# Weight sums of a Winograd-form squared-ReLU layer: sign changes, and two of four sums made by accumulating DMA transfers

## The chip, the cores and the metric

The kernel runs on one core of a Trainium2 chip. The core has a matrix engine (TensorE, "PE" in the profile, with its weight loads as "PEld"), a vector engine (VectorE, "DVE"), an activation engine (ScalarE, "ACT"), a general engine (GpSimd, "POOL") and a synchronisation engine (SyncE, "SP") that here issues nearly all DMA transfers. The metric is device time in microseconds (us) of one execution.

## The reference

A trunk of two residual layers on 512 tokens of width 1024, all in float32. Layer 0 mixes tokens with chunked band attention, layer 1 with a gated linear recurrence. Behind each mixer stands a dense squared-ReLU layer, which is what the change is about:

```python
def sq_relu_mlp(h, w1, w2):
    z = jax.nn.relu(jnp.einsum('bsd,df->bsf', h, w1))
    return jnp.einsum('bsf,fd->bsd', z * z, w2)

def reference(x, norm_mix, norm_mlp, ...):
    h = x
    for layer in range(DEPTH):
        hn = rmsnorm(h, norm_mix[layer])
        ...
        h = h + mix
        h = h + sq_relu_mlp(rmsnorm(h, norm_mlp[layer]), mlp_w1[layer], mlp_w2[layer])
    return rmsnorm(h, norm_final)
```

The hidden width is 4096, so `w1` is 1024 x 4096 and `w2` is 4096 x 1024.

## The kernel before

**Precision.** A float32 product is made of three matmuls of a reduced format (float32r): each operand is rounded to a high part, and what is left over is its low part. So every unit of weights, 128 partitions by 1024 elements (512 KB), is loaded by a transfer of SP, rounded by ScalarE (line 141, tile `wh`), and its low part is formed by VectorE (line 144, tile `wl`). A function `fetch` does this for the next unit of a written-out list, `plan`. `want` hands units to TensorE in that order, and fetches until five units (four outside these layers, three in a last round) are ready beyond those it hands out.

**The squared-ReLU layer.** The second product is done in four rounds `p`. A round takes 1024 rows of `w2` and all its 1024 columns, as four blocks of 512 x 512: "11" and "12" are the left and right columns of the first 512 rows, "21" and "22" those of the second. The activations of the round form four blocks too: two halves of the tokens (256 each) by two halves of the rows. With four blocks a side the round uses Winograd's form of Strassen's product: seven block products in place of eight, paid for with sums of blocks. On the activations' side these are `s1` to `s4` (lines 686 and 730 to 733). On the weights' side they are

- t1 = 12 - 11, written over block 12,
- t2 = 22 - t1, written over block 22 after block 22 itself has been used,
- t3 = t2 - 11, written over block 11,
- t4 = 21 - t2, written over block 21.

Each is made by VectorE in two halves (128 x 1024 elements each) at line 139, in `fetch`, right before the rounding cast of that half. The blocks are loaded by SP at line 129, eight transfers of 512 KB a round, when `fetch` comes to the unit "11". Each of the four blocks has one buffer (tags `b11`, `b21`, `b12`, `b22`), so a load waits until the round before has done with it. The buffers of "12" and "22" first hold the residual, turned, at the start of a layer (`turn`, line 636: 32 small transfers), and only then the first round's blocks.

**The order of the work.** In a round TensorE computes the second half of the first product's columns (`up`, j = 4 to 7), then the seven products: "11", "21" (with the activations' "12"), t1, "22", t2, t3, t4. Between the last four it computes the first half of the next round's columns (`ahead`), except in the last round. The activations come out of PSUM through a ReLU and a square on ScalarE (lines 655 and 656), and each block or sum of them is split into high and low part (`split`, lines 679 and 680). Products are read back from PSUM by VectorE (`read`, line 643) as d = acc x r + d, where r is the per-token factor of the norm, `rq`. The engines each run their own queue in order. What stands in what order in a queue is decided when the program is built, by a planner that goes by its own costs, and the order of the source breaks ties. GpSimd has no work in these layers.

Of the kernel before, what the change touches and what calls it, by code (L numbers as in the profile page):

```python
# [10 lines left out]
F32 = mybir.dt.float32  # L11
F32R = mybir.dt.float32r
AF = mybir.ActivationFunctionType
ALU = mybir.AluOpType

P = 128
# [5 lines left out]
U = 256  # L22
# [13 lines left out]
def f(ap):  # L36
    return ap.bitcast(F32)
# [3 lines left out]
def trunk(ctx: ExitStack, tc: tile.TileContext, xT, cols, gfin, win, wqkv, wo, rwin, rga, rgx, rwo, w1, w2, out):  # L41
    nc = tc.nc
    V, S, G, PE = nc.vector, nc.scalar, nc.gpsimd, nc.tensor

    per = ctx.enter_context(tc.tile_pool(name="per", bufs=1))
# [6 lines left out]
    def mmp(name):  # L52
        return ps.tile([P, T], F32, name=name, tag="mm")
# [20 lines left out]
    spare = per.tile([P, 1], F32, name="spare")  # L74
    rt = per.tile([P, 4], F32, name="rt")
    rq = per.tile([P, 4], F32, name="rq")
    fs = per.tile([P, 8], F32, name="fs")
    sp4 = per.tile([P, KT], F32, name="sp4")
    sp8 = per.tile([P, KT], F32, name="sp8")
# [19 lines left out]
    raws, start_ = {}, []  # L99

    def fetch():
        i = state["next"]
        state["next"] += 1
        kind, nk, srcs = plan[i]
        pool = wsp
        if state["more"] is not None and i < state["end"]:
            pool = state["more"] if state["units"] % 7 >= 5 else wsp
            state["units"] += 1
        H = pool.tile([P, 1024], F32R, name=f"wh{i}", tag="wh")
        L = pool.tile([P, 1024], F32R, name=f"wl{i}", tag="wl")  # L110
        n = 1024
        if kind == "plain":
            n = nk * sum(src.shape[1] for src in srcs)
            raw = wraw.tile([P, 1024], F32, name=f"wr{i}", tag="wr")
            rv = raw[:, :n].rearrange("p (k c) -> p k c", k=nk)
            c0 = 0
            for n_, src in enumerate(srcs):
                w = src.shape[1]
                queue = nc.scalar if i == 0 and n_ else nc.sync
                queue.dma_start(rv[:, :, c0 : c0 + w], src.rearrange("(k p) c -> p k c", p=P))  # L120
                c0 += w
        else:
            half, nk = nk, 2
            if kind == "11" and half == 0:
                for name, src in zip(("11", "21", "12", "22"), srcs):
                    both = state["raw"].tile([P, 2, 1024], F32, name=f"b{name}_{i}", tag=f"b{name}")
                    for h in range(2):
                        raws[name, h] = both[:, h]
                        nc.sync.dma_start(
                            raws[name, h].rearrange("p (k c) -> p k c", k=2),  # L130
                            src[h * U : (h + 1) * U].rearrange("(k p) c -> p k c", p=P),
                        )

            at_, x, y = {
                "t1": ("12", "12", "11"), "t2": ("22", "22", "12"), "t3": ("11", "22", "11"), "t4": ("21", "21", "22"),
            }.get(kind, (kind, None, None))
            raw = raws[at_, half]
            if x:
                V.tensor_sub(raw, raws[x, half], raws[y, half])  # L139
        if i:  # L140
            S.copy(H[:, :n], raw[:, :n])  # L141
        else:
            start_.append(V.tensor_copy(H[:, :n], raw[:, :n]))
        low = V.tensor_sub(L[:, :n], raw[:, :n], f(H[:, :n]))  # L144
        if not i:
            start_.append(low)
        state["ready"].append((nk, H[:, :n].rearrange("p (k c) -> p k c", k=nk), L[:, :n].rearrange("p (k c) -> p k c", k=nk)))

    def prefetch(n):
        while len(state["ready"]) < n and state["next"] < len(plan) and state["next"] != state["stop"]:  # L150
            fetch()

    def want(n):
        prefetch(n + state["ahead"])
        got = [state["ready"].pop(0) for _ in range(n)]
        nk = got[0][0]
        return (lambda k, c: got[k // nk][1][:, k % nk, c]), (lambda k, c: got[k // nk][2][:, k % nk, c])
# [64 lines left out]
    def project(accs, cols_, WH, WL, xs, first=True, last=True):  # L222

        for k, (XH, XL) in enumerate(xs):
            for acc, c in zip(accs, cols_):
                mm3(acc, WH(k, c), WL(k, c), XH, XL, first and k == 0, last and k == len(xs) - 1)
# [383 lines left out]
    def mlp(ly, norm):  # L610
        with ExitStack() as mctx:
# [6 lines left out]
            dt = {(t, c): res[:, t, c] for t in range(4) for c in range(2)}  # L618
# [6 lines left out]
            def turn():  # L625
                blocks = [sr.tile([P, 2, 4, KT, 32], F32, name=f"turned{ly}{h}", tag=f"b{n}2") for h, n in enumerate((1, 2))]
                for k in range(KT):
                    for h in range(2):
                        V.transpose(
                            blocks[h].rearrange("p t j k a -> p (t j) k a")[:, :, k],  # L630
                            hT[k][:, h * U : (h + 1) * U].rearrange("p (n b) -> p n b", b=32),
                        )
                for h in range(2):
                    for i in range(4):
                        for j in range(4):
                            nc.sync.dma_start(
                                res[32 * j : 32 * j + 32, 2 * h : 2 * h + 2, i // 2, (i % 2) * U : (i % 2 + 1) * U],
                                blocks[h][32 * i : 32 * i + 32, :, j].rearrange("p t k a -> p t (k a)"),
                            )

            def read(acc, t, c):
                d, r = dt[t, c], rq[:, t : t + 1]
                V.scalar_tensor_tensor(d, acc, r, d, ALU.mult, ALU.add)  # L643


# [2 lines left out]
            def up(p, j):  # L648
                if j % 4 == 0:
                    a[p, j // 4] = zp.tile([P, 2, 4, U], F32, name=f"a{ly}{p}{j}", tag=f"a{j // 4}")  # L650
                WH, WL = want(1)
                acc = mmp(f"u{ly}{p}{j}")
                project([acc], [slice(0, P)], WH, WL, xs)
                c = a[p, j // 4][:, :, j % 4, :]
                S.activation(c, acc.rearrange("p (h c) -> p h c", h=2), AF.Relu)  # L655
                S.activation(c, c, AF.Square)  # L656
                if (p, j) == (0, 0):
                    turn()
                if (p, j) == (0, 5):
                    for t in range(4):  # L660
                        for c in range(2):
                            squares(t, c)
                if (p, j) == (0, 6):
                    V.tensor_add(rq, fs[:, 0:8:2], fs[:, 1:8:2])
                    V.tensor_scalar(rq, rq, 1.0 / D, EPS, ALU.mult, ALU.add)
                    V.reciprocal(rq, rq)

            def round_(p):
                A, low, raw = {}, {}, {}
# [7 lines left out]
                def split(n, ks=slice(0, 4)):  # L677
                    H, L = low[n]
                    S.copy(H[:, ks], raw[n][:, ks])  # L679
                    V.tensor_sub(L[:, ks], raw[n][:, ks], f(H[:, ks]))  # L680
# [33 lines left out]
                def step(name, bank, fresh, t0, c):  # L714
                    apart = p == 3 and name != "12"
                    if not apart:
                        product(name, bank, fresh)
                    for t in range(2):
                        if apart:
                            product(name, bank, fresh, ts=(t,))  # L720
                        read(bank[t], t0 + t, c)

                chunks = {5: slice(0, 2), 7: slice(2, 4)} if p < 3 else {5: slice(0, 2), 6: slice(2, 3), 7: slice(3, 4)}
                for j in range(4, 8):
                    up(p, j)
                    raw["12"], raw["22"] = a[p, 1][:, 0], a[p, 1][:, 1]
                    if j in chunks:
                        ks = chunks[j]
                        r = {n: raw[n][:, ks] for n in raw}
                        V.tensor_sub(r["s2"], r["22"], r["s3"])  # L730
                        V.tensor_sub(r["s4"], r["12"], r["s2"])
                        split("12", ks)
                        V.tensor_add(r["s1"], r["s1"], r["22"])

                    if j == (5 if p == 3 else 7):
                        step("11", X, True, 0, 0)
# [33 lines left out]
            def squares(t, c):  # L770
                sq = wk.tile([P, T], F32, name=f"dsq{ly}{t}{c}", tag="nsq", bufs=2)
                S.activation(sq, dt[t, c], AF.Square, accum_out=part(t, c))
# [93 lines left out]
            for j in range(4):  # L866
                up(0, j)
# [11 lines left out]
    def open_x(u):  # L879
        WH, WL = want(1)  # L880
        for i in range(2):
            xbs.append(mmp(f"xb{2 * u + i}"))
            project(xbs[-1:], PAIR[i : i + 1], WH, WL, [(hnH[k], hnL[k]) for k in range(4, KT)], last=False)
            yield

    mlp(0, nm1)


    nm2 = Norm("nm2", C_MLP1, late=True)
    with ExitStack() as rctx:  # L890
# [83 lines left out]
        for u in range(4):  # L974
            WH, WL = want(2 if u > 1 else 1)
            for i in range(2):
                c = 2 * u + i
# [19 lines left out]
        for u in range(4):  # L997
            WH, WL = want(2)
            for i in range(2):
                c = 2 * u + i  # L1000
# [32 lines left out]
        for u in range(2, 4):  # L1033
            WH, WL = want(2)
            for i in range(2):
                m = 2 * u + i
                project([accs[m]], PAIR[i : i + 1], WH, WL, [gd[k] for k in range(KT)])
                ro_out(m)

    mlp(1, nm2)  # L1040


# [39 lines left out]
```

## Time and profile before

| | us |
|---|---|
| runs shown: median (lowest to highest) | 1053.89 (1053.03 to 1054.12) |
| the profiled execution's span, first to last instruction | 1052.7 |
| TensorE busy in it | 1042.4 |
| VectorE busy | 809.2 |
| ScalarE busy | 583.4 |
| GpSimd busy | 9.4 |
| line 139, the weight sums: 64 instructions on VectorE | 76.4 |
| weight blocks of `w2`: 64 transfers of 512 KB, median to landing | 5.6 |

The profiled execution's own time is given by its span alone. The median of the runs is 1.2 us above it. Layer 0's squared-ReLU layer takes the span from about 230 to 570 us, layer 1's from about 715 to the end. A round lasts about 82 us. In the timeline's rows the columns are the start in us, the duration in us, the engine, the line, the operation, the tile written and those read, shapes, and in brackets the engine's idle time just before with what ended it. In rows of groups the numbers behind the bar are busy time in us and the mean of one in ns, then the idle time before them.

### The profile page before, as it was taken

The page shows a single profiled execution, that of the slowest core. Times are in us where ns is not written, and L with a number is a line of the kernel's source. Part 1 is how long each engine was busy: PE and PEld are TensorE (multiplying, and loading weights), DVE is VectorE, ACT ScalarE, POOL GpSimd, SP SyncE. Part 2 cuts the span into 40 slices and gives each one's busy share as a digit, 9 for nine tenths or more (in the row PEclk, how much of TensorE's full clock was granted, in tenths as well). Part 3 has the DMA queues.
Part 4 walks back from the last instruction along what each step waited for, and adds up shares of the span by engine and source line. Part 5 has one row for each costly group of instructions (what it writes and reads, how often), then busy time and mean ns, then how long its engine had stood idle before and what let it go on. Part 6 is the DMA issues. An engine that isn't in the chain of part 4 may idle for free.

```text
span 1052.7 us, 12888 instructions
## 1 busy us (share of the span) xinstructions
PE 1042.4 (99%) x4754; PEld 863.3 (82%) x4754; DVE 809.2 (77%) x1218; ACT 583.4 (55%) x906; POOL 9.4 (1%) x28
## 2 busy tenths in 40 slices
PE   9999999999999999999999999999999999999997
PEld 8788888888888888888888888888888888888886
DVE  7898779867597687587599888985597587487596
ACT  7676567644564454454456786544554454454454
POOL 1000000000000000000000000000000000000000
PEclk9999999999999999999999999999999999999999
DMA  8444353243636026125103312164536026125002
GB/s 267 116 125 136 81 161 119 61 155 105 182 100 201 20 81 201 39 79 185 57 1 105 116 60 82 60 209 127 183 100 202 18 82 201 39 80 180 1 1 80
DMA packets 133535, 115.72 MB, mean 110 GB/s; under 512 B 5344, under 2 KB 109792, under 8 KB 133472
## 3 DMA queue, kind: packets, MB, share of 16 engines
q1 hardware_dynamic: 132896, 114.18, 35.5%
q8 instruction: 37, 0.61, 0.2%
q10 hardware_dynamic: 576, 0.72, 0.2%
q14 instruction: 26, 0.21, 0.1%
HBM read 104.39 MB, written 2.10 MB: 101 GB/s over the span
## 4 chain that ended last, share of the span: by engine, by line
PE 96%; DVE 2%; ACT 1%; issue 1%; DMA 0%; POOL 0%; DVEq 0%; ACTq 0%; POOLq 0%
PE u L220 11%; PE u L218 11%; PE u L219 11%; PE x L218 6%; PE x L220 6%; PE x L219 6%; PE y L218 3%; PE y L220 3%; PE y L219 3%; PE x L447 2%; PE wo L218 1%; PE wo L219 1%; PE ro L220 1%; PE ro L218 1%; PE wo L220 1%; PE xb L218 1%
## 5 line engine op out<-in xcount | busy, mean ns | idle before, releaser
L141 ACT CAST wh<-b 128x1024 fp32r<-128x1024 f32 x112 | 117.7, 1052 | 158.4 <-PE u L219 105.8
L144 DVE TENSOR_TENSOR wl<-wr,wh 128x1024 fp32r<-128x1024 f32 (+1 forms) x122 | 146.2, 1200 | 76.3 <-ACT wh L141 75.9
L141 ACT CAST wh<-wr 128x1024 fp32r<-128x1024 f32 (+1 forms) x121 | 125.7, 1040 | 140.3 <-PE u L219 60.4
L218 PE MATMUL u<-hnH,wh 128*128 128x512 f32 x512 | 199.2, 389 | 0.0
L220 PE MATMUL u<-hnH,wl 128*128 128x512 f32 x512 | 199.2, 389 | 0.0
L219 PE MATMUL u<-hnL,wh 128*128 128x512 f32 x512 | 199.2, 389 | 0.0
L144 DVE TENSOR_TENSOR wl<-b,wh 128x1024 fp32r<-128x1024 f32 x112 | 136.4, 1220 | 79.4 <-ACT wh L141 79.1
L219 PEld LDWEIGHTS u<-hnL,wh 128*128 128x128 f32 x512 | 96.1, 188 | 20.2
L220 PEld LDWEIGHTS u<-hnH,wl 128*128 128x128 f32 x512 | 96.1, 188 | 19.9
L218 PEld LDWEIGHTS u<-hnH,wh 128*128 128x128 f32 x512 | 96.1, 188 | 19.9
L139 DVE TENSOR_TENSOR b<-b,b 128x1024 f32<-128x1024 f32 x64 | 76.4, 1217 | 0.7 <-DMA b<-in_w 0.5
L655 ACT ACTIVATE a<-u 128x512 f32<-128x512 f32 x64 | 37.9, 591 | 32.2 <-PE u L220 32.2
L218 PE MATMUL x<-wh,h 128*128 128x512 f32 (+1 forms) x132 | 50.9, 385 | 0.6 <-DVE d L852 0.6
L219 PE MATMUL x<-wl,h 128*128 128x512 f32 (+1 forms) x132 | 50.6, 383 | 0.0
L643 DVE SCALAR_TENSOR_TENSOR d<-x,rq,d 128x512 f32<-128x512 f32 x63 | 44.8, 743 | 2.3 <-PE x L220 2.3
L656 ACT ACTIVATE a<-a 128x512 f32<-128x512 f32 x64 | 40.5, 633 | 1.8
L427 ACT ACTIVATE p<-p,mx 128x128 f32<-128x128 f32 (+1 forms) x64 | 35.2, 552 | 6.1 <-DVE mx L424 5.8
L679 ACT CAST h<-a 128x1024 fp32r<-128x1024 f32 (+2 forms) x34 | 27.2, 800 | 7.6 <-PE y L219 6.7
L420 DVE CUSTOM_DVE_ANT_0 p<-s,bias 128x128 f32<-128x128 f32 (+1 forms) x64 | 27.9, 484 | 3.6 <-PE s L417 3.3
L451 ACT CAST pH<-x 128x512 fp32r<-128x512 f32 (+1 forms) x48 | 21.8, 516 | 13.9 <-PE x L447 13.8
L218 PEld LDWEIGHTS x<-wh,h 128*128 128x128 f32 x132 | 24.8, 188 | 5.5 <-DVE d L852 0.8
L219 PEld LDWEIGHTS x<-wl,h 128*128 128x128 f32 x132 | 24.8, 188 | 4.8
(340 smaller groups left out, 2281.4 us busy)
## 6 DMA issues: line engine op xcount, KB each, us to landing
wr<-in_w SPq DMA_DIRECT2D x64, 512.0 KB, 4.1
b<-in_w SPq DMA_DIRECT2D x64, 512.0 KB, 5.6
wr<-in_wqkv SPq DMA_DIRECT2D x20, 512.0 KB, 3.9
wr<-in_rwin SPq DMA_DIRECT2D x16, 512.0 KB, 3.3
wr<-in_wo SPq DMA_DIRECT2D x8, 512.0 KB, 3.6
d<-turned SPq DMA_DIRECT2D x64, 64.0 KB, 2.0
wr<-in_rwo SPq DMA_DIRECT2D x8, 512.0 KB, 3.4
x<-in_xT SPq DMA_DIRECT2D x8, 256.0 KB, 4.0
```

Of the source, the lines that this page charges most:

```text
L139: V.tensor_sub(raw, raws[x, half], raws[y, half])
L141: S.copy(H[:, :n], raw[:, :n])
L144: low = V.tensor_sub(L[:, :n], raw[:, :n], f(H[:, :n]))
L218: PE.matmul(acc, WH, XH, start=start, stop=False, skip_group_check=more)
L219: PE.matmul(acc, WH, XL, start=False, stop=False, skip_group_check=more)
L220: PE.matmul(acc, WL, XH, start=False, stop=stop, skip_group_check=more)
L420: V.tensor_tensor_reduce(out=pt[:, seg[t] : seg[t] + n], in0=sc[t], in1=b[:, h % 4, T - n :], scale=1.0, scalar=-3.0e38, op0=ALU.add, op1= ...
L427: S.activation(pt[:, seg[t] : seg[t] + n], pt[:, seg[t] : seg[t] + n], AF.Exp, bias=mx[:, t : t + 1], accum_out=sm[:, t : t + 1],)
L643: V.scalar_tensor_tensor(d, acc, r, d, ALU.mult, ALU.add)
L655: S.activation(c, acc.rearrange("p (h c) -> p h c", h=2), AF.Relu)
L656: S.activation(c, c, AF.Square)
L679: S.copy(H[:, ks], raw[n][:, ks])
```

## The change

The signs of the second half of the activations' rows, of the second half of the weights' rows and of the right-hand columns are turned in thought, so that the sums on the weights' side become t1 = 12 + 11, t2 = 22 + t1, t3 = t2 - 11, t4 = 21 + t2. On the activations' side s1, s2 and s4 change signs, s2 and s4 with a three-operand instruction instead of a subtraction. The right-hand columns of the result come out negated, so `read` uses a second factor, `nrq` = -`rq`, for them.

Two of the four sums are then made by transfers that add to what is at their destination, issued by GpSimd. t1: block 11 is read a second time from DRAM and added to block 12 in SBUF, once 12 has landed. t4: t2 is read from SBUF and added to block 21 in SBUF. t2 and t3 stay on VectorE.

```diff
+    nrq = per.tile([P, 4], F32, name="nrq")
...
-                for name, src in zip(("11", "21", "12", "22"), srcs):
+                blocks = dict(zip(("11", "21", "12", "22"), srcs))
+
+                def rows(name, h):
+                    return blocks[name][h * U : (h + 1) * U].rearrange("(k p) c -> p k c", p=P)
+
+                for name in blocks:
                     both = state["raw"].tile([P, 2, 1024], F32, name=f"b{name}_{i}", tag=f"b{name}")
                     for h in range(2):
                         raws[name, h] = both[:, h]
-                        nc.sync.dma_start(
-                            raws[name, h].rearrange("p (k c) -> p k c", k=2),
-                            src[h * U : (h + 1) * U].rearrange("(k p) c -> p k c", p=P),
-                        )
-
-            at_, x, y = {
-                "t1": ("12", "12", "11"), "t2": ("22", "22", "12"), "t3": ("11", "22", "11"), "t4": ("21", "21", "22"),
-            }.get(kind, (kind, None, None))
-            raw = raws[at_, half]
-            if x:
-                V.tensor_sub(raw, raws[x, half], raws[y, half])
+                        nc.sync.dma_start(both[:, h].rearrange("p (k c) -> p k c", k=2), rows(name, h))
+                for h in range(2):
+                    G.dma_start(raws["12", h].rearrange("p (k c) -> p k c", k=2), rows("11", h), accum_op=ALU.add)
+
+            raw = raws[{"t1": "12", "t2": "22", "t3": "11", "t4": "21"}.get(kind, kind), half]
+            if kind == "t2":
+                V.tensor_add(raw, raw, raws["12", half])
+            if kind == "t3":
+                V.tensor_sub(raw, raws["22", half], raw)
+            if kind == "t4":
+                G.dma_start(raw, raws["22", half], accum_op=ALU.add)
...
-                d, r = dt[t, c], rq[:, t : t + 1]
+                d, r = dt[t, c], (nrq if c else rq)[:, t : t + 1]
...
                     V.reciprocal(rq, rq)
+                    V.tensor_scalar(nrq, rq, -1.0, None, ALU.mult)
...
-                        V.tensor_sub(r["s2"], r["22"], r["s3"])
-                        V.tensor_sub(r["s4"], r["12"], r["s2"])
+                        V.scalar_tensor_tensor(r["s2"], r["22"], -1.0, r["s3"], ALU.mult, ALU.subtract)
+                        V.scalar_tensor_tensor(r["s4"], r["12"], -1.0, r["s2"], ALU.mult, ALU.subtract)
                         split("12", ks)
-                        V.tensor_add(r["s1"], r["s1"], r["22"])
+                        V.tensor_sub(r["s1"], r["22"], r["s1"])
```

## The prediction

> **What bounds the kernel now.** I read the page first, then the engines' busy time by stretches, then what TensorE waited for.
>
> ```profile
> span 1052.7 us, 12888 instructions
> ...
> PE 1042.4 (99%) x4754; PEld 863.3 (82%) x4754; DVE 809.2 (77%) x1218; ACT 583.4 (55%) x906; POOL 9.4 (1%) x28
> ...
> PE   9999999999999999999999999999999999999997
> ...
> PE 96%; DVE 2%; ACT 1%; issue 1%; DMA 0%; POOL 0%; DVEq 0%; ACTq 0%; POOLq 0%
> ```
>
> TensorE is busy for all but 1052.7 - 1042.4 = 10.3 us, and 96% of the chain that ended last is TensorE. The next rows say where those 10.3 us lie (columns: stretch, then busy us and instruction count for each engine). The last two rows are from a finer cut.
>
> ```profile
> 0.00:30.00 30.00, 28.96 (x129) 24.30 (x130) 23.51 (x29) 20.78 (x30) 3.49 (x13) 1.00 0.78 248
> 30.00:240.00 210.00, 207.04 (x1054) 173.16 (x1053) 176.82 (x427) 131.24 (x296) 5.92 (x15) 1.00 0.41 119
> ...
> 300.00:400.00 100.00, 100.00 (x442) 82.78 (x442) 79.62 (x110) 49.69 (x58) 0.00 (x0) 1.00 0.34 106
> ...
> 500.00:570.00 70.00, 70.00 (x317) 57.79 (x316) 55.31 (x63) 37.94 (x51) 0.00 (x0) 1.00 0.14 45
> ...
> 1000.00:1052.70 52.70, 46.37 (x214) 38.27 (x212) 43.90 (x65) 27.27 (x47) 0.00 (x0) 0.96 0.11 40
> ```
>
> ```profile
> 270.00:280.00 10.00, 10.00 (x46) 8.29 (x45) 3.59 (x3) 5.31 (x11) 0.00 (x0) 1.00 0.72 223
> ...
> 310.00:320.00 10.00, 10.00 (x46) 8.27 (x45) 10.00 (x10) 5.34 (x6) 0.00 (x0) 1.00 0.23 70
> ```
>
> 1.0 us is idle in the start, 3.0 in attention, 6.3 in the last stretch, which holds the final normalisation. Inside the squared-ReLU layers TensorE has no idle time at all. It also doesn't run slower when VectorE is full: 46 matmuls in the 10 us in which VectorE worked 3.59, and 46 in the 10 us in which it worked all 10.00. So there is no slack in these layers that a lighter VectorE could turn into time. TensorE's own waits after the start confirm it:
>
> ```profile
> PE s L416 <- DVE mx L420: 2.4, 1, 2.4
> PE x L218 <- DVE d L852: 0.6, 1, 0.6
> PE s L416 <- DMA kl<-kl: 0.4, 1, 0.4
> ```
>
> Only the 0.6 us belongs to a squared-ReLU layer, in the tail, which the change leaves as it is.
>
> **The change part by part: VectorE.** Of 64 weight sums, 32 (t1 and t4, two halves each, in 8 rounds) leave it. 18 sums of the activations in each layer become three-operand instructions, dearer by the difference of the two rows below them.
>
> ```profile
> L139 DVE TENSOR_TENSOR b<-b,b 128x1024 f32<-128x1024 f32 x64 | 76.4, 1217 | 0.7 <-DMA b<-in_w 0.5
> ...
> L643 DVE SCALAR_TENSOR_TENSOR d<-x,rq,d 128x512 f32<-128x512 f32 x63 | 44.8, 743 | 2.3 <-PE x L220 2.3
> ```
>
> ```profile
> L730 DVE TENSOR_TENSOR fs<-a,cs 128x512 f32<-128x512 f32 x2 | 1.4, 692 | 4.4 <-ACT a L656 4.4
> ```
>
> Removed: 32 x 1.217 = 38.9 us. Added: at most 36 x (0.743 - 0.692) = 1.8 us, and two 128x4 negations, less than 0.7 us each by the same row. VectorE falls by some 36 us, all of it beside TensorE: worth 0 on the path. The signs of the other sums and the negated scale in the read-out change no count and no size. The 0.05 us that the three-operand form adds ahead of a split of the activations has 4.6 us of cover (worked out below).
>
> **The transfers.** GpSimd issues 32 accumulating transfers of 512 KB. It executes nothing in these layers (x0 above), so what is queued behind a waiting transfer is only the next accumulating one. SP's loads are not behind it. t1 now waits for its block 12 to land and then for an accumulate. t4 waits for t2, as before, and then for an accumulate. Behind each on ScalarE stands, in order, the rounding cast of that unit; behind the cast stand ReLUs and splits that TensorE needs sooner than the weights themselves. That is the one road to TensorE.
>
> No accumulate is in this trace. Its nearest rows are the plain transfers (the issues with their median to landing, then min/median/max of the weight blocks, then the rate in 40 slices of 270 to 310 us):
>
> ```profile
> b<-in_w SPq DMA_DIRECT2D x64, 512.0 KB, 5.6
> ...
> d<-turned SPq DMA_DIRECT2D x64, 64.0 KB, 2.0
> ```
>
> ```profile
> DMA to landing us min/median/max: 3.3/5.6/8.1
> ```
>
> ```profile
> GB/s 127 80 129 66 201 334 324 274 324 369 375 348 351 324 339 137 4 0 0 0 0 0 35 173 305 11 0 0 0 0 0 65 268 208 0 0 0 133 358 377
> ```
>
> From below, a pair of halves is no quicker than one plain block, 3.3 us. From above, each half reads two streams at the pace of the slowest block, one after the other: 2 x 2 x 8.1 = 32.4 us. My value: fixed part 2.0 us (the small transfer) plus twice the block's remainder, 2 x (5.6 - 2.0), is 9.2 us for the first half. The second follows on the same engines after two more streams of 512 KB at about 350 GB/s, 3.0 us. So 12.2 us for a pair. I take that rather than an end because the engines are full when it matters, as in the median block.
>
> The Trainium skill, "DMA: Bandwidth & Descriptors", section "Anatomy of one DMA — SWDGE (gpsimd) path", fits a transfer from GpSimd at 2.0 us plus bytes over 436 GB/s, and "Collectives: The Full Stack", section "The bandwidth ceiling", says that an add in the DMA path costs a second read and not the addition. By the two an accumulate of 512 KB would be an estimated 4.4 us and a pair about 7; no run here shows it, and the sum would be the same, since that is shorter than my value.
>
> **The tightest place is t1 of the first round of each layer**, because its block 12 is loaded late, after the transfers of the turned residual that use the same buffer. Issue and landing of blocks 12 and 22 in the two layers, then the casts of t1's second half and the cast behind them, the split that ends that chain on VectorE, and the matmul that needs it:
>
> ```profile
> L129 SPq DMA_DIRECT2D b<-in_w x4: 368/473/576, 272.9 to 274.8; - x4
> ...
> DMA to landing us min/median/max: 3.8/6.1/7.2
> ```
>
> ```profile
> L129 SPq DMA_DIRECT2D b<-in_w x4: 368/537/608, 742.4 to 744.1; - x4
> ...
> DMA to landing us min/median/max: 5.3/6.3/7.5
> ```
>
> ```profile
> 284.20 1.06 ACT L141 CAST wh<-b 128x1024 fp32r<-128x1024 f32 x1 [2.04 <-DVE b L139]
> ...
> 285.65 1.04 ACT L141 CAST wh<-b 128x1024 fp32r<-128x1024 f32 x1
> ...
> 289.36 1.05 ACT L141 CAST wh<-wr 128x1024 fp32r<-128x1024 f32 x1 [2.14 <-PE u L219]
> ```
>
> ```profile
> 292.26 0.69 DVE L680 TENSOR_TENSOR nn<-a,h 128x512 fp32r<-128x512 f32 x1
> ```
>
> ```profile
> 297.55 0.39 PE L218 MATMUL z<-wh,h 128*128 128x512 f32 x1
> ```
>
> ```profile
> 759.44 1.03 ACT L141 CAST wh<-b 128x1024 fp32r<-128x1024 f32 x1
> 762.68 1.05 ACT L141 CAST wh<-wr 128x1024 fp32r<-128x1024 f32 x1 [2.21 <-PE u L219]
> ```
>
> ```profile
> 765.59 0.69 DVE L680 TENSOR_TENSOR nn<-a,h 128x512 fp32r<-128x512 f32 x1
> ```
>
> ```profile
> 770.87 0.39 PE L218 MATMUL z<-wh,h 128*128 128x512 f32 x1
> ```
>
> First layer: block 12's second half is issued near 273.4 and lands at 273.4 + 6.1 = 279.5. The cast of t1's second half starts at 285.65. It can slip by ScalarE's idle 2.14 us behind it and by the 297.55 - 292.95 = 4.6 us between the split's end and its matmul, so to 285.65 + 6.74 = 292.4, before TensorE loses anything. Budget for the pair: 12.9 us. With 12.2 it is there at 291.7. Second layer: lands at 742.9 + 6.3 = 749.2; the cast may slip to 759.44 + 2.21 + 4.59 = 766.2: a budget of 17.0 us. Cost in both: 0, with 0.7 us to spare in the first. Without that cover each microsecond beyond the budget is one on TensorE.
>
> **t4, and t1 in later rounds.** t2's second half starts on VectorE, t4's second half is cast, and the matmuls take it (a middle round, then the last round, where the first of three sums is t2's second half):
>
> ```profile
> 304.95 1.22 DVE L139 TENSOR_TENSOR b<-b,b 128x1024 f32<-128x1024 f32 x1
> ```
>
> ```profile
> 324.95 1.05 ACT L141 CAST wh<-b 128x1024 fp32r<-128x1024 f32 x1 [0.74 <-PE x L220]
> ```
>
> ```profile
> 343.79 0.39 PE L218 MATMUL x<-wh,h 128*128 128x512 f32 x1
> ```
>
> ```profile
> 1011.08 3.62 DVE L139 TENSOR_TENSOR b<-b,b 128x1024 f32<-128x1024 f32 x3
> ```
>
> ```profile
> 1029.22 1.06 ACT L141 CAST wh<-b 128x1024 fp32r<-128x1024 f32 x1 [0.79 <-PE y L220]
> ```
>
> From t2's end at 306.2 the cast is 18.8 us away and the matmuls 37.6; in the last round 1029.2 - 1012.3 = 16.9 us. 12.2 us fits. t1 of a later round has more: block 12 is free again once t2 has read it at 306.2, and the sum is due only in the round after. **Sum:** 0 on TensorE's path, so the profiled 1052.7 us plus the 1.2 us by which the median 1053.89 exceeds that span: 1053.9 us.
>
> **The rivals.** (1) *Accumulates are late in the first round, slower.* Point from which it decides: a pair beyond 12.9 us. At 20 us a pair costs 7.1 in the first layer and 3.0 in the second: 1064.0. At the upper bound of 32.4, 19.5 + 15.4: 1088.8. For it: my value lies 0.7 us inside the budget, and the rate row shows full engines from 275 to 285. Against: the pair may overlap, and a cast that is planned behind the ReLU need only meet the weights' own due time, several microseconds later.
>
> (2) *The planner's order changes.* A cast or a load is placed elsewhere because a sum became a transfer, and a few gaps open in a TensorE row that has none. Against: five units of weights are ready ahead. Price: one or two weight sums' lateness in each layer, at 1.2 us by L139's row, 2.4 to 4.9 in all: 1056.3 to 1058.8.
>
> (3) *Descriptors held up by VectorE.* If GpSimd can't write them while VectorE works, the transfer starts in VectorE's next gap: in the first layer that begins at 290.45 - 2.50 = 287.95, and the pair lands 12.2 us later at 300.2, 7.8 beyond the limit: 1061.7 with the first layer alone.
>
> ```profile
> 290.45 1.23 DVE L144 TENSOR_TENSOR wl<-wr,wh 128x1024 fp32r<-128x1024 f32 x1 [2.50 <-ACT wh L141]
> ```
>
> The Trainium skill, "SBUF — State Buffer", section "Who interferes with whom", has this rule for VectorE's two-port modes and takes two-input instructions, which these sums are, out of it for descriptor writing, as an inference; no run here shows it.
>
> (4) *Faster.* The 36 us of VectorE would have to shorten something. The only TensorE wait in reach is 0.6 us: 1053.3, which is no measurable gain. More needs a pitch that depends on VectorE, and 46 against 46 speaks against it.
>
> **Chances.** Differences within 0.2%, 2.1 us, are taken as no change. Forecast 0.70, and (4) at 0.6 us or sums that don't leave VectorE 0.02 with it: same 0.72. (1) 0.14, (2) 0.07, (3) 0.04: slower 0.25. Faster by over 2.1 us, by something not seen here: 0.03. The forecast's own range is 1052.0 to 1056.0. To hold 8 in 10 the range reaches on over (2) and (3) and the nearer part of (1): 1052.0 to 1062.0. It leaves out the pairs beyond 18 us.
>
> **What would show it.** Right: 32 rows of L139's kind fewer on VectorE, TensorE's stretches still at 100.00 of 100, casts of t1 in the first rounds behind a DMA for some microseconds, and no TensorE wait that leads back to them. Wrong: a TensorE idle stretch near 292 to 305 or 766 to 780 whose release goes by a cast to an accumulate (1), gaps spread over rounds without a transfer at their head (2), GpSimd's transfers starting only at VectorE's gaps (3), or a TensorE that does the same matmuls in less time (4).

## The result, and the profile after

The changed kernel takes 1060.73 us (median; 1058.49 to 1061.61), the kernel before 1054.01 us in the same comparison. The ratio is 1.0059, with a 95% interval of 1.0047 to 1.0070: the change costs 6.2 us, between 5.0 and 7.4. The profiled execution's span went from 1052.7 to 1059.8 us, 7.1 more; that execution, 1061.61 us, is the longest of the four of the kernel after.

The page of the kernel after: span, engines, the two groups of accumulating transfers (each with 512 KB), and the time from issue to landing of the loads and the accumulates.

```profile
span 1059.8 us, 12976 instructions
...
PE 1046.6 (99%) x4754; PEld 865.8 (82%) x4754; DVE 775.9 (73%) x1188; ACT 583.1 (55%) x906; POOL 42.9 (4%) x60
...
L137 POOL DMA_DIRECT2D b<-in_w x16 | 19.7, 1231 | 409.1 <-DMA b<-in_w 321.9
...
L145 POOL DMA_DIRECT2D b<-b x16 | 14.2, 889 | 407.1 <-DVE b L141 398.8
...
b<-in_w POOLq DMA_DIRECT2D x16, 512.0 KB, 8.5
b<-b POOLq DMA_DIRECT2D x16, 512.0 KB, 5.3
```

VectorE is relieved by 809.2 - 775.9 = 33.3 us (some 36 were foreseen), in 30 instructions fewer. TensorE has the same 4754 matmuls but needs 4.2 us more for them (1046.6 against 1042.4), and is idle for 13.2 us in place of 10.3. Its waits over the whole span (us in total, times, the longest) show one that the kernel before did not have:

```profile
PE y L226 <- DVE ls L687: 2.8, 2, 2.0
```

Both times it is the matmul that takes the low part of the sum `s1`, once in the first round of each squared-ReLU layer. In the first layer this is TensorE (start, duration):

```profile
301.90 0.39 PE L225 MATMUL y<-wl,h0s 128*128 128x512 f32 x1
304.32 0.50 PE L226 MATMUL y<-wh,ls 128*128 128x512 f32 x1 [2.03 <-DVE ls L687]
...
305.88 0.63 PE L226 MATMUL y<-wh,ls 128*128 128x512 f32 x1
306.31 0.63 PE L224 MATMUL y<-wh,h0s 128*128 128x512 f32 x1
...
309.24 0.39 PE L225 MATMUL y<-wl,h0s 128*128 128x512 f32 x1
309.47 0.40 PE L226 MATMUL y<-wh,ls 128*128 128x512 f32 x1
```

Two things are lost here. First the wait: the matmul with `ls` started at 300.72 before and starts at 304.32 now, 3.60 later. At 290 us TensorE is 0.9 later than before, so 2.7 us go: 2.2 to 2.3 in the wait, and about 0.4 just ahead of it, from 298 us on, where the matmuls that take the split `nn` are late by the same chain (that split ends at 299.13, the first of them starts at 299.18). Then, from 305.88 to 309.24, eight matmuls follow each other at some 0.43 us; before and after that stretch it is 0.23. That is 8 x 0.2, so 1.6 us more. The windows (busy us and count of PE, PEld, DVE, ACT, POOL, then the granted clock) say what it is:

```profile
300.00:310.00 10.00, 7.97 (x28) 5.90 (x27) 9.74 (x11) 4.34 (x5) 0.00 (x0) 0.83 0.31 90
310.00:320.00 10.00, 10.00 (x46) 8.29 (x45) 10.00 (x11) 5.83 (x7) 3.00 (x3) 1.00 0.83 175
```

The granted clock of that window is 0.83, and 1.00 in the next. The wait alone was 2.0 us; the lower clock came on top.

Followed matmul by matmul, the 7.1 us lie as follows: 0.9 before 290 us; 4.5 from 298 to 310 us, the stretch just shown; 0.4 between 310 and 607 us; 1.0 in the first round of the second layer; 0.3 after it. The first item isn't the change's. Most of it comes at 43 to 47 us, in attention, before any accumulate, where the granted clock is 0.83 in the window from 40 to 50 us and 1.00 in the kernel before (these rows stand further below); the profiles of two kernels below, with more room and with t4 alone, have it too, and their medians are those of before. What stands for the change is 4.5 + 1.0, and the median's 6.2 to 6.7 is about 1 us more than that; I come back to it.

### Where the wait comes from

The chain back from the matmul goes over VectorE and ScalarE to GpSimd. The split of `s1`, the two casts of t1 and the cast behind them (timelines of the kernel after):

```profile
303.05 1.21 DVE L687 TENSOR_TENSOR ls<-a,h0s 128x1024 fp32r<-128x1024 f32 x1
```

```profile
288.60 1.05 ACT L147 CAST wh<-b 128x1024 fp32r<-128x1024 f32 x1 [2.96 <-DMA b<-in_w]
...
294.47 1.05 ACT L147 CAST wh<-b 128x1024 fp32r<-128x1024 f32 x1 [4.29 <-DMA b<-in_w]
295.43 1.04 ACT L147 CAST wh<-wr 128x1024 fp32r<-128x1024 f32 x1
```

ScalarE waits 2.96 us for the first half of t1 and 4.29 us for the second, and everything behind it moves. GpSimd's own timeline and the landings of the two (min/median/max):

```profile
279.02 1.35 POOL L137 DMA_DIRECT2D b<-in_w  x1 [108.54 <-DMA b<-in_w]
288.78 1.24 POOL L137 DMA_DIRECT2D b<-in_w  x1 [8.41 <-issue]
310.70 0.91 POOL L145 DMA_DIRECT2D b<-b  x1 [20.68 <-DVE b L141]
313.01 0.86 POOL L145 DMA_DIRECT2D b<-b  x1 [1.40 <-ACT h0s L686]
```

```profile
DMA to landing us min/median/max: 5.6/7.6/9.5
```

The first accumulate goes out at 279.02, as soon as its block is there, and lands 9.5 us later, at 288.5. The second goes out at 288.78, right after that landing, and lands at 294.4. In between GpSimd is idle for 8.41 us, and the profile calls it "issue": it shows nothing that GpSimd waited for. The two accumulates of t4 (line 145), in contrast, go out 2.3 us apart. So the pair of t1 takes 15.4 us, not because the engines are slow but because its second half starts late.

### The profile page after: what moved, and what is told of

Same layout as the page of the kernel before. It is cut to its first block, busy times and chain, and to the rows that moved or that the text cites. A ratio compares the mean times of both kernels' runs of the same rounds, so it can differ in the third digit from the quotient of the medians.

```text
span 1059.8 us, 12976 instructions
## 1 busy us (share of the span) xinstructions
PE 1046.6 (99%) x4754; PEld 865.8 (82%) x4754; DVE 775.9 (73%) x1188; ACT 583.1 (55%) x906; POOL 42.9 (4%) x60
## 4 chain that ended last, share of the span: by engine, by line
PE 62%; DVE 3%; DMA 2%; issue 2%; SPq 2%; ACT 1%; POOL 0%; ACTq 0%; DVEq 0%; POOLq 0%
PE u L224 8%; PE u L225 8%; PE u L226 8%; PE x L224 5%; PE x L226 5%; PE x L225 5%; PE y L226 3%; PE y L224 3%; PE y L225 3%; SPq L642 2%; DMA b<-in_w 2%; PE ro L225 1%; PE ro L224 1%; PE ro L226 1%; PE yb L226 1%
## 5 line engine op out<-in xcount | busy, mean ns | idle before, releaser
L137 POOL DMA_DIRECT2D b<-in_w x16 | 19.7, 1231 | 409.1 <-DMA b<-in_w 321.9
L145 POOL DMA_DIRECT2D b<-b x16 | 14.2, 889 | 407.1 <-DVE b L141 398.8
L226 PE MATMUL y<-wh,ls 128*128 128x512 f32 x64 | 26.1, 407 | 2.8 <-DVE ls L687 2.8
```

What stands on the lines that cost most here:

```text
L226: PE.matmul(acc, WL, XH, start=False, stop=stop, skip_group_check=more)
```

## The experiments

After this reading the theory was: the kernel reserves little room for the descriptors that GpSimd writes (`dynamic_dma_scratch_size=1024`, line 1071 of the kernel before, untouched by the change), and one accumulate of t1 leaves no place for the next. Rivals: accumulates of GpSimd always run one after the other; the loss comes from the sign changes or from t4; the matmuls at half pace come from the accumulates' traffic and not from TensorE's idle time.

**More room, nothing else.** The order of every queue stays as in the kernel after.

```diff
-dynamic_dma_scratch_size=1024
+dynamic_dma_scratch_size=1920
```

> The changed kernel with one number altered: the room for GpSimd's transfer descriptors, 1024 bytes of a partition, becomes 1920. Theory A (the pair of t1 is late because GpSimd starts the second half only when the first has landed, for want of descriptor room): in the first rounds the second transfer starts within 2 us of the first, in place of 9.8 (279.0 to 288.8) and 9.1 us later (754.7 to 763.8); the cast of t1's second half comes at or before 291 in place of 294.5; TensorE loses none of the 4.5 us of the first layer nor the 1.0 us of the second; 1054 to 1055.5 us. Theory B (the engines are full, and two transfers at once only slow each other): the second lands within 1.5 us of where it landed, 294.4, TensorE still waits, and the time stays at 1059 to 1061. Theory C (the planner's order is what costs): the order of all queues is that of the changed kernel, so the time stays at 1059 to 1061.

Measured: 1054.74 us, ratio to before 1.0006 (0.9998 to 1.0015), as theory A had it; only the cast came 1.3 us later than it said (292.33, not 291), 0.6 us of which this whole trace is behind that of the kernel after. GpSimd, the landings, ScalarE's second cast of t1, the split of `s1` and its matmul:

```profile
279.46 1.35 POOL L137 DMA_DIRECT2D b<-in_w  x1 [108.30 <-DMA b<-in_w]
281.48 1.21 POOL L137 DMA_DIRECT2D b<-in_w  x1 [0.67 <-DMA b<-in_w]
```

```profile
DMA to landing us min/median/max: 9.7/10.2/10.8
```

```profile
292.33 1.05 ACT L147 CAST wh<-b 128x1024 fp32r<-128x1024 f32 x1 [1.55 <-DMA b<-in_w]
```

```profile
300.91 1.21 DVE L687 TENSOR_TENSOR ls<-a,h0s 128x1024 fp32r<-128x1024 f32 x1
```

```profile
302.24 0.44 PE L226 MATMUL y<-wh,ls 128*128 128x512 f32 x1
```

The second accumulate now goes out 2.0 us after the first and waits for its own half block only. The pair lands 12.8 us after its start. The split of `s1` ends at 302.12, 0.12 us before TensorE takes it, and TensorE doesn't wait. One number of the program's set-up holds all of the loss that stands out from the noise. It also shows how narrow the place is: with every obstacle gone, a tenth of a microsecond is left.

**How much room.** The same edit with 1152.

> The changed kernel with 1152 bytes of a partition for the descriptors in place of 1024, an eighth more. If a pair of added transfers needs just over what 1024 bytes hold (16 rows an engine and half, read from two places, so 32 reads and something for the completion, twice that being a little over 64 entries of 16 bytes): the second half starts within 2 us of the first and the time is that of the wide room, 1054 to 1055.5 us. If a transfer wants much more room, or the start hangs on another thing that 1920 bytes changed: the second half starts about 9 us later, as with 1024, and the time is 1059 to 1061.

Measured: 1055.03 us, ratio 1.0009 (1.0000 to 1.0018).

```profile
279.00 1.36 POOL L137 DMA_DIRECT2D b<-in_w  x1 [108.17 <-DMA b<-in_w]
280.87 1.21 POOL L137 DMA_DIRECT2D b<-in_w  x1 [0.51 <-DMA b<-in_w]
```

An eighth more room is enough: the two go out 1.9 us apart, and TensorE has no wait for `ls`. A pair of accumulates of t1, 512 KB each from DRAM, needs more than 1024 and no more than 1152. The pair of t4, from SBUF, fits into 1024: in the kernel after it went out 2.3 us apart, with a median of 5.3 us to landing, so both halves were under way at once.

**Is it any two transfers of GpSimd?** The transfers of t1 write block 11 over block 12 without adding; this leaves out the addition of t1, so the weights of that product are other numbers.

```diff
-... rows("11", h), accum_op=ALU.add)
+... rows("11", h))
```

> The changed kernel without the addition in t1's transfers: GpSimd writes block 11 over block 12 instead of adding it, so t1 and what follows from it is another sum. Same order in all queues. Theory A (descriptor room, of which an added transfer needs more because it reads two streams): the second half starts within 2 us of the first, a transfer takes less than the 9.5 us of the first half, 5 to 8 us beside the other loads, and the time is 1053.5 to 1055.5. A rival (any two of GpSimd's transfers go one after the other): the second still starts when the first has landed, the pair takes 11 to 14 us.

Measured: 1054.82 us, ratio 1.0008 (0.9999 to 1.0017). Both go out at once, in one row:

```profile
278.61 1.64 POOL L137 DMA_DIRECT2D b<-in_w  x2 [109.62 <-ACT a L661]
```

```profile
DMA to landing us min/median/max: 7.3/7.7/8.1
```

With the room of 1024, two plain transfers of t1 fit beside each other; two adding ones don't. Each also keeps GpSimd only 0.77 to 0.88 us (1.21 to 1.35 with the add). So an adding transfer takes more room than a plain one of the same size. The pair lands within 9.0 us (279.5, the second's issue, + 8.1 at most), against 12.8 with the add and room enough: at least 3.8 us for the add, both beside the same loads.

**Which part of the change.** All four sums on VectorE with the new signs; then t1 alone by transfers; then t4 alone; then t1 by transfers in all rounds but the first of each layer.

t4 back on VectorE (signs only, and t1 alone):

```diff
-                G.dma_start(raw, raws["22", half], accum_op=ALU.add)
+                V.tensor_add(raw, raw, raws["22", half])
```

t1 back on VectorE (signs only, and t4 alone):

```diff
-                for h in range(2):
-                    G.dma_start(raws["12", h]..., rows("11", h), accum_op=ALU.add)
+            if kind == "t1":
+                V.tensor_add(raw, raw, raws["11", half])
```

t1 back on VectorE in the first round of each layer, by a counter of the rounds:

```diff
-                for h in range(2):
+                state["round"] = state.get("round", -1) + 1
+                for h in range(2 if state["round"] % 4 else 0):
+            if kind == "t1" and state["round"] % 4 == 0:
+                V.tensor_add(raw, raw, raws["11", half])
```

> The signs of the changed kernel alone: all four weight sums stay on VectorE as additions and one subtraction, GpSimd issues nothing in the layers. Theories A and B (the transfers cost): as before the change, within 0.15%, 1053 to 1055.5 us, TensorE at 100.00 of 100 in the layers. Theory C (a changed order or the dearer three-operand sums): slower by at least 2 us.

> t1 by transfers as in the change, t4 back on VectorE. Theories A and B (t1 of the first rounds costs all of it): as the changed kernel, 1059 to 1061.5 us, with TensorE's wait of about 2 us near 302 in the first layer. If t4's transfers had a part: nearer to before by what that part is.

> t4 by transfers as in the change, t1 back on VectorE. Theories A and B: as before the change, 1053 to 1055.5 us, since t4 is needed 17 us or more after its start and lands in 5 to 6. If t4's transfers cost anything: slower than that by at least 1 us, with a TensorE wait behind a cast of the last units of a round.

> The changed kernel, but in the first round of each layer t1 is made by VectorE; the other three rounds of each layer make it by GpSimd's transfers, with the small descriptor room, so that the second half still starts late there. Theory A (only the first rounds have too little time): 1053.5 to 1055.5 us, as before the change, with second transfers still starting 9 us after the first in the later rounds and no TensorE wait. A rival (every late pair costs something): 3 us or more of the 6.7 remain.

| | us | ratio to before (95%) |
|---|---|---|
| signs only | 1054.20 | 1.0002 (0.9994 to 1.0011) |
| t1 by transfers | 1060.70 | 1.0065 (1.0052 to 1.0078) |
| t4 by transfers | 1054.13 | 1.0003 (0.9994 to 1.0011) |
| t1 and t4, but t1 not in the first rounds | 1054.28 | 1.0006 (0.9997 to 1.0015) |

t1 alone has the whole loss, with the same rows: 10.5 us between the two issues, and the wait for `ls` in both layers.

```profile
279.58 1.34 POOL L137 DMA_DIRECT2D b<-in_w  x1 [108.29 <-DMA b<-in_w]
290.06 1.23 POOL L137 DMA_DIRECT2D b<-in_w  x1 [9.14 <-issue]
```

```profile
PE y L226 <- DVE ls L687: 3.1, 2, 2.0
```

In the last kernel of the table t1's pairs of the later rounds are still held apart, by 9.1 us here, and nothing waits for them:

```profile
312.00 1.24 POOL L138 DMA_DIRECT2D b<-in_w  x1 [4.95 <-ACT a L664]
321.13 1.21 POOL L138 DMA_DIRECT2D b<-in_w  x1 [7.89 <-issue]
```

In the kernel after the second half starts late in all eight rounds, 8.5 to 9.9 us behind the first; it costs something only in the two in which the block is loaded late.

**Is the slow stretch TensorE's idle time, or the transfers?** In the kernel before, which has no accumulates, VectorE gets extra instructions that rewrite `s1` with itself ahead of its split, in the first round of the first layer. First four and six of them:

```diff
+                if (ly, p) == (0, 0):
+                    for _ in range(N):
+                        V.scalar_tensor_tensor(raw["s1"], raw["s1"], 1.0, raw["s1"], ALU.mult, ALU.min)
```

> The kernel before, with 4 further VectorE instructions of about 1.25 us each in the first round of the first layer, which rewrite the sum s1 with itself ahead of its split. The split's low part is due 2.7 us after it ends now, so TensorE should stand idle for about 2.3 us. Theory T (a wait of 2 us or more makes TensorE's clock fall for some microseconds after it): the time rises by the wait and some 2.4 us more, 1058 to 1059. Theory N (the slow matmuls near 306 us in the changed kernel have another cause, its transfers): it rises by the wait alone, about 1056.2.

> The same with 6 such instructions: a wait of about 4.8 us. Theory T: the wait and at least as much more as with 4, 1061 to 1063. Theory N: the wait alone, 1058.7.

Measured: 1054.03 us (1.0001; 0.9992 to 1.0010) with four and 1055.64 us (1.0021; 1.0012 to 1.0030) with six. Both expectations missed: the planner put the next columns' matmuls ahead of the late product, so TensorE waited not at all and for 0.8 us, and the clock was not put to the test. The edit was then repeated with TensorE's order held: the first matmul behind the one that takes `s1` is told to stay behind it, without a wait of its own.

```diff
-        PE.matmul(acc, WH, XH, start=start, stop=False, skip_group_check=more)
+        opens = PE.matmul(acc, WH, XH, start=start, stop=False, skip_group_check=more)
+        if state.get("hold") is not None:
+            after(opens, state.pop("hold"))
...
-        PE.matmul(acc, WL, XH, start=False, stop=stop, skip_group_check=more)
+        state["last"] = PE.matmul(acc, WL, XH, start=False, stop=stop, skip_group_check=more)
...
+                if (ly, p) == (0, 0):
+                    state["hold"] = state["last"]
```

> The kernel before with 2 further VectorE instructions of about 1.2 us ahead of the split of s1 in the first round of the first layer, and with TensorE's order held, so that the next columns' matmuls can't step in front of that product. TensorE should wait about 1 to 2 us near 301 us. Theory T (the clock falls only behind a wait of about 2 us): under 1.5 us of wait the time rises by the wait alone; matmuls stay 0.227 us apart. Theory N (the slow matmuls of the changed kernel come from its transfers): the same.

> The kernel before with 3 further VectorE instructions ahead of the split of s1 in the first round of the first layer, TensorE's order held: a wait between the nearly nothing of 2 and the 4.9 us of 5, about 1.5 to 2.5 us. The changed kernel waited 2.03 us there and its matmuls then stood 0.427 us apart for 3.4 us. Theory T (the wait alone is the cause): from about 2 us of wait matmuls stand 0.427 us apart for a stretch that starts within 2 us behind it, and the time rises by the wait and 1 to 3 us more; with a wait of 1.1 us or less, none. Theory N (it takes GpSimd's transfers too, or a wait over 3 us): no slow matmuls at 2 us, the time rises by the wait alone.

> The same with 5 such instructions: a wait of about 4 to 6 us. Theory T: behind the wait matmuls stand 0.427 us apart for some microseconds, the granted clock of that stretch is below 0.9, and the time rises by the wait and at least 2 us more, 1060 to 1063. Theory N: matmuls 0.227 us apart right behind the wait, and the time rises by the wait alone, 1058 to 1060.

| extra instructions | us | ratio to before (95%) | TensorE's waits there, us | matmuls at half pace |
|---|---|---|---|---|
| 2 | 1054.07 | 1.0002 (0.9993 to 1.0010) | none listed | none |
| 3 | 1056.46 | 1.0024 (1.0014 to 1.0034) | 0.84 and 0.64 | none |
| 5 | 1061.06 | 1.0066 (1.0054 to 1.0078) | 4.91 | from 307.05 to 313.33 |

TensorE with three, then with five, and the two windows with five:

```profile
301.35 0.50 PE L218 MATMUL y<-wh,h0s 128*128 128x512 f32 x1 [0.84 <-ACT h0s L681]
...
303.20 0.74 PE L222 MATMUL y<-wh,ls 128*128 128x512 f32 x2 [0.64 <-DVE ls L682]
303.77 0.40 PE L218 MATMUL y<-wh,h0s 128*128 128x512 f32 x1
304.01 0.39 PE L221 MATMUL y<-wl,h0s 128*128 128x512 f32 x1
```

```profile
307.05 0.80 PE L218 MATMUL y<-wh,h0s 128*128 128x512 f32 x1 [4.91 <-ACT h0s L681]
...
312.90 0.60 PE L221 MATMUL y<-wl,h0s 128*128 128x512 f32 x1
313.33 0.41 PE L222 MATMUL y<-wh,ls 128*128 128x512 f32 x1
```

```profile
300.00:310.00 10.00, 5.09 (x17) 3.51 (x16) 10.00 (x11) 2.60 (x3) 0.00 (x0) 0.83 0.00 0
310.00:320.00 10.00, 10.00 (x39) 8.08 (x38) 9.22 (x9) 4.10 (x4) 0.00 (x0) 0.83 0.51 159
```

With five the half pace is there, in a kernel without accumulates, in a window in which the DMA engines moved nothing (share 0.00) and GpSimd did nothing. So it needs no accumulate: TensorE's idle time is enough to bring it. With three there are two waits of less than a microsecond and no half pace; matmul by matmul they cost 2.1 of the 2.6 us by which the median rose. The waits expected with two and with three instructions (1 to 2 us, and 1.5 to 2.5 us) didn't come, so these two runs say nothing about a wait of 2 us.

How long a wait must be can't be said either, because its length alone doesn't decide. Every profile has one such wait in attention, near 42 us and before any accumulate. This is the kernel before, then the kernel after, each with its window:

```profile
42.88 0.50 PE L416 MATMUL s<-kl,q 128*128 128x512 f32 x1 [2.44 <-DVE mx L420]
```

```profile
40.00:50.00 10.00, 7.51 (x37) 5.67 (x36) 7.42 (x31) 6.95 (x21) 0.00 (x0) 1.00 0.30 85
```

```profile
42.58 0.52 PE L422 MATMUL s<-kl,q 128*128 128x512 f32 x1 [1.77 <-DVE mx L426]
```

```profile
40.00:50.00 10.00, 8.23 (x32) 6.66 (x31) 7.49 (x31) 7.04 (x22) 0.00 (x0) 0.83 0.30 79
```

A wait of 2.44 us left the clock whole in the kernel before, and one of 1.77 us was followed by half pace in the kernel after. Of the fourteen profiles six show 0.83 in this window, behind waits of 1.77 to 2.42 us, and eight show 1.00, behind waits of 1.28 to 2.44 us. So in attention none of the waits of up to 1.31 us was followed by half pace, and between 1.77 and 2.44 us both happened. What decides between the two, these runs don't show.

The lengths of the slow stretches are alike: a window of 10 us with a clock of 0.83 holds 0.17 x 10 / 0.5 = 3.4 us at half clock. There is one such window behind the 2.03 us of the kernel after, and there are two behind 4.91 us.

The Trainium skill, "TensorE: Matmul & The Clock Gate", section "Part 1: The HAM clock gate (the "warmup" mystery)", has the clock halved after an idle window of some 3.4 us, on a window that runs freely. The halved pace (0.43 us against 0.23) and the 3.4 us for which it lasted agree, and a window that runs freely fits waits of about 2 us that end in both ways. But waits of 1.77 to 2.42 us, shorter than such a window, were enough in these profiles, and the measurement decides.

## Where the prediction was right and where it was wrong, point by point

**The measured 1060.73 us lies within the stated 1052.0 to 1062.0, and that is largely luck.** The range was drawn to reach over rivals (2) and (3) and the nearer part of (1), and (1) is what happened. But by (1)'s own rule the pair of 15.4 us that came is worth 1056.4 us; what carried the time on to 1060.7 was not in the prediction: a tighter limit, the clock, and about a microsecond that has no place yet. (By the same rule the bound of 1062.0 belongs to a pair of 19.0 us, not of 18.)

**The forecast (no change, 1053.9) failed and rival (1), late accumulates in the first round, happened.** The place was right, the chain to it (accumulate, cast, what stands behind the cast) too, and the row that was to show it (an idle stretch near 292 to 305 that leads back to a cast and an accumulate) is the one that appeared. Three steps between were wrong.

**"The second follows on the same engines after two more streams ... 3.0 us."** This step decided the case. The first half was valued at 9.2 us and took 9.5. The second was taken to be in flight beside it; it was issued 9.8 us after it, and the pair took 15.4 us instead of 12.2. With room for the descriptors the pair measured 12.8, so the 12.2 was a fair size for what it assumed. What the step lacked is a resource: the room in which GpSimd writes its descriptors, which a plain pair didn't fill and the adding pair did. The trace of before could not show it, with no transfers from GpSimd in these layers; the setting stood in the program, and it was not among the rivals. Rival (3) also held descriptors up, but by VectorE's work. VectorE, however, was idle for 5.14 us up to 289.69, that is from 284.55 on, and the second accumulate still went out only at 288.78; with more room it went out as soon as its own block was there. So nothing of that kind shows.

```profile
289.69 1.23 DVE L150 TENSOR_TENSOR wl<-b,wh 128x1024 fp32r<-128x1024 f32 x1 [5.14 <-ACT wh L147]
```

**The budget of 12.9 us.** It was read at the split of block 12 of the activations (`nn`), which has 4.6 us of cover. A later split on the same queue has less. The rows of before:

```profile
296.82 1.22 DVE L680 TENSOR_TENSOR ls<-a,h0s 128x1024 fp32r<-128x1024 f32 x1
```

```profile
300.72 0.39 PE L220 MATMUL y<-wh,ls 128*128 128x512 f32 x1
```

The split of `s1` ends at 298.0, its matmul comes at 300.72: 2.7 us of cover, and 0.2 of VectorE's idle time on the way. So the cast could slip to 285.65 + 2.14 + 2.9 = 290.7, not 292.4, and the budget from 279.5 was 11.2 us. Even the predicted 12.2 us, counted from there, would have been 1 us late. The kernel with more room tests the limit: its cast at 292.33, in a trace that runs 1.5 us behind the one of before at this place, is at 290.8 in the times of before, and 0.12 us remained. Its pair of 12.8 us could just fit because the start was wrong too, in the other direction: 279.5 is the landing of block 12's second half, but the first accumulate waits for the first half alone and went out at 279.46, which is 278.0 in the times of before. The step that failed is the choice of the split: the cover was taken from the first instruction behind the stall, not from the one with the least.

Second layer, by the same rows of the kernel after:

```profile
754.72 1.21 POOL L137 DMA_DIRECT2D b<-in_w  x1 [208.84 <-DMA b<-in_w]
763.83 1.23 POOL L137 DMA_DIRECT2D b<-in_w  x1 [7.90 <-issue]
```

```profile
769.83 1.05 ACT L147 CAST wh<-b 128x1024 fp32r<-128x1024 f32 x1 [5.19 <-DMA b<-in_w]
770.79 0.59 ACT L661 ACTIVATE a<-u 128x512 f32<-128x512 f32 x1
771.41 0.63 ACT L662 ACTIVATE a<-a 128x512 f32<-128x512 f32 x1
```

The budget of 17.0 us should have held, with a pair of about 15.1 us, but TensorE waited 0.7 us. Here also the tighter split counts, with the same 2.9 us by this layer's rows: the cast may slip to 759.44 + 2.21 + 2.9 = 764.5. And behind the late cast stood a ReLU and a square, 1.2 us, which the kernel before has ahead of it, as the first layer still has; that leaves 763.4. The cast at 769.83, in a trace 5.7 us behind, is at 764.1: 0.7 late.

**"Each microsecond beyond the budget is one on TensorE."** The cast was about 2.9 us beyond the true limit (294.47, in a trace 0.9 us behind, against 290.7), and the wait with what went just ahead of it cost 2.7. So far the rule held. But the granted clock then took 1.6 us more: 4.3 us for 2.9 of lateness. The prediction had no term for what TensorE's idle time does to the matmuls behind it; the trace of before, with 2.44 us of waiting in attention and no half pace behind it, gave no sign of one.

**What held.** VectorE's relief was valued at nothing, and the kernel with more room, with all of it, is not faster than before (1.0006). t4 was valued at nothing: 1.0003 alone. Later rounds of t1: nothing, though their pairs are late as well. The sign changes: nothing (1.0002). Rival (2), the planner's order: the order around the cast did change a little (a square moved ahead of it in the first layer, a ReLU and a square behind it in the second, where by the sum above the cast would have been in time without them), but with the same order and more room the loss is gone.

**What stays open.** The two first rounds make 5.5 us in the profiled execution, which is the longest of its four; the median is 6.2 to 6.7 us above. The executions differ in their mean granted clock: 1061.61 us at 0.995, 1060.84 and 1060.62 at 0.997, 1058.49 at 0.999. One stretch of 3.4 us at half clock is worth 0.5 x 3.4 / 1060, so 0.0016 of the mean clock and 1.7 us. The differences fit one such stretch more or less, but only the profiled execution was followed matmul by matmul, so this isn't shown, and about a microsecond has no place. With t1 alone it is much the same (1059.11 us at 0.999 to 1063.61 at 0.995). The way in which descriptors fill the room wasn't observed either; that room decides is shown by the edit of that one number.

No version is better than the kernel before: TensorE is busy in these layers all the time, so taking up to 33 us from VectorE with the stall removed left 1054.74 against 1053.88 us.

## What to carry to other kernels

When work moves to a queue that was idle, look for the resources that only that queue uses (here the room for GpSimd's descriptors), since the trace of before has no row for them; a pair of transfers costed as overlapping needs a reason why the second may start. For the cover of a stall, walk the queue behind it to the instruction with the least slack, not to the first; and where the engine behind it is TensorE at its full clock, allow for a lower clock behind the idle time: here it came behind some waits of about 2 us and not behind others. And an engine that has no idle time gains nothing from relief elsewhere, so such an edit has only a downside to be worked out.

## What the runs showed of the hardware

- Two adding transfers of 512 KB from DRAM held each other apart (9.1 to 10.5 us between issues in the first rounds) with a room of 1024, and went out 1.9 us apart with 1152; two plain ones fitted into 1024. The profile has no name for this wait but "issue".
- An accumulate of 512 KB took 8.5 us from DRAM and 5.3 us inside SBUF (medians), and GpSimd 1.23 and 0.89 us to issue it. The Trainium skill's pages "DMA: Bandwidth & Descriptors", section "Anatomy of one DMA — SWDGE (gpsimd) path", and "Collectives: The Full Stack", section "The bandwidth ceiling", from which the prediction estimated 4.4 us for one and about 7 us for a pair, give less than every one of these: the pair measured 12.8 us with room and 15.4 without, beside other loads.
- A wait of 2.03 us was followed, 1.6 us after TensorE had begun again, by eight matmuls at half pace. Length alone doesn't decide: waits of up to 1.31 us were not followed by it, 1.77 us was and 2.44 us wasn't.
